# Three of four token parts of a final RMSNorm summed by a matrix of ones, and the scaling moved into the last matmul chains

## The chip, the cores and the metric

The kernel runs on one core of one Trainium2 chip. The metric is the device time of one execution in microseconds, as the median of several runs. One execution was also profiled; its trace is what the argument works from.

## The reference, cut to what matters

One decoder layer (attention with a 128-token window, a gated MLP branch, a ConvFFN) for 1024 prompt tokens and 64 sample tokens, and a final RMSNorm. The part that the change touches is the end:

```python
def rmsnorm(x, g):
    xf = x.astype(jnp.float32)
    y = xf * lax.rsqrt(jnp.mean(xf * xf, axis=-1, keepdims=True) + EPS)
    return (y * g.astype(jnp.float32)).astype(x.dtype)
...
    x = x + merged @ w_out
    f, nconv = conv_ffn(rmsnorm(x, norm_ffn), w_up, conv_w, conv_b, w_down, conv_prev)
    return x + f, nk, nv, nconv, vn
...
    y_prompt = rmsnorm(xp, norm_final)
    y_sample = rmsnorm(xs, norm_final)
```

D is 1024, the ConvFFN is 2816 wide, everything is float32.

## The kernel before, in words

Activations lie transposed: 128 channels on the partitions, tokens along the free axis. The 1088 tokens (64 sample, 1024 prompt) are two halves of 544 (`th` 0 and 1); the 1024 channels are 8 tiles of 128, in two halves of 4 tiles (`dh` 0 and 1, tile `m` 0 to 3 in each). To keep float32 accuracy every operand is split into a rounded high plane and a low rest (`split`, line 41: ScalarE copies the high plane, VectorE subtracts), and each product is three matmuls: high by high, high by low, low by high.

**Up-projection.** Two-by-two block products are done with seven instead of eight products (`Chain.product`, line 310). Token group 0 (576 tokens, two halves of 288 columns) reads four T tiles `t0` to `t3`, each `[128, 7, 2, 288]` with seven sums and their two planes; group 1 (two halves of 256 columns) reads `th`/`tl` tiles. The T tiles of group 0 come from `both_planes`, one tile at a call, with 64 bytes of gap (`line(pool, 64)`) behind each. A tile is 16128 bytes, 63 times 256, so one gap of 64 shifts a tile's start by 64 against a multiple of 256. They are made twice, for the input projection and for the up-projection.

**Down-projection.** Again seven products in the order `DN_ORDER = (5, 0, 2, 4, 6, 1, 3)`, here called stages 0 to 6. Each stage has 11 units (`NU`); a unit is a half weight tile (`wh`, `wl`, 128x512) and a token operand (`th`, `tl`, 128x544), and gives 24 matmuls (4 tiles `m`, two column spans `e` of 288 and 256, three terms; `mm_dn`, line 1679). `units` asks ahead: it has token operands split up to unit x+2 and weights split two units ahead of the one in use (`W.get(2, ...)`). A stage's sums are in six PSUM banks `dn` and are taken into the residual `x1[dh, th, e]` on VectorE (`take`, line 1689). Token half 0 is complete after stage 4, half 1 with channel half 1 after stage 5, and the last stage finishes half 1 with channel half 0.

**The last four units** run as chains: span e=0 with m 0 to 3, each 12 matmuls, then span e=1 likewise. A chain's end lets `take` and the squares (`square`, line 1698) follow.

**Final norm.** It is done for four parts `(th, e)`. `square` sums squares over channel tiles into `acc` (VectorE, line 1701). `fin_rms` (line 1712) reduces over the partitions with small matmuls (`acc` as weights, one column of ones), takes the root on ScalarE and the reciprocal of a few columns on VectorE; `fin_rb` (line 1724) spreads the result over the partitions by matmuls with an identity; `fin_mul` copies that to SBUF (ScalarE, line 1732) and multiplies: VectorE with the gain from PSUM (line 1749), GpSimd from SBUF (line 1751). Parts (0,0) and (0,1) are reduced ahead of unit 8 of stage 5 and unit 0 of stage 6, and multiplied ahead of units 2 and 3 of stage 6 (`hooks[at, lo]`). Part (1,0) is reduced and multiplied inside the e=1 chains. Part (1,1) comes last, with three matmuls of ones ahead of its end (line 1837). Every part leaves by DMAs from the SyncE queue (`y_out`, line 1737).

A scheduler orders the instructions of each engine. An instruction under `tc.keep_in_program_order` keeps its place among the others so marked.

Of the kernel before, what the change touches and what calls it, by code (L numbers as in the profile page):

```python
# [15 lines left out]
P = 128  # L16
D = 1024
KD = 8
# [16 lines left out]
def layer(tc, a):  # L35
    nc = tc.nc
    V, S, G, PE = nc.vector, nc.scalar, nc.gpsimd, nc.tensor
# [11 lines left out]
    with ExitStack() as top:  # L49
# [12 lines left out]
        eps = cst.tile([P, 1], F32, name="c_eps")  # L62
# [182 lines left out]
        W = Weights(top.enter_context(tc.tile_pool(name="wp", bufs=2)), 4, 4)  # L245
# [16 lines left out]
        def both_planes(pool, name):  # L262
            t = pool.tile([P, 7, 2, 288], F32R, name=name)
            line(pool, 64)
            return t[:, :, 0], t[:, :, 1]

        def combine(t4, b11, b12, b21, b22, eng=G):
# [108 lines left out]
        with ExitStack() as ph1:  # L376
            c1 = ph1.enter_context(tc.tile_pool(name="c1", bufs=1))
# [61 lines left out]
            early = set(range(NPRE, FEW))  # L439
# [199 lines left out]
            t0h, xr = right(th0, "T0h"), right(xro, "xr")  # L639
            txa = [{}, {}]  # L640
# [20 lines left out]
            def t0_job(kk):  # L661
                def go():
                    first, t4, rest = sums_of(0, kk)
                    txa[0][kk] = th, tl = both_planes(t0h, f"t{kk}")
# [287 lines left out]
            for at, (pair, gs) in enumerate(seq):  # L952
# [12 lines left out]
                for j in range(7):  # L965
                    w = W.get(3, 1 if j < 4 else 4 if at == len(seq) - 1 else 2)
# [407 lines left out]
            for c in range(KD):  # L1374
                xt = x_next(0, c)
                w, ps = W.get(), acc2()
# [9 lines left out]
            t0p = right(t0o, "T0")  # L1386
# [38 lines left out]
            def t0_split(kk):  # L1425

                def go():
                    x0, x1, t4 = hx.pop(kk)
                    tx[0][kk] = th, tl = both_planes(t0p, f"t0{kk}")
# [24 lines left out]
        def t_upto(loads, splits):  # L1454

            for n in range(len(ts["raw"]), min(loads, 7 * (NFF // 2))):
                j, i = DN_ORDER[n // (NFF // 2)], n % (NFF // 2)
                raw = dnp["t"].tile([P, 576], F32, name="traw", bufs=4)[:, :HT]
                nc.sync.dma_start(raw, td[i][:, T_AT[j]])
                ts["raw"].append(raw)  # L1460
            for n in range(len(ts["made"]), min(splits, 7 * (NFF // 2))):
                th, tl = (dnp["t"].tile([P, 576], F32R, name=x, bufs=5)[:, :HT] for x in ("th", "tl"))
                if n == 0:
                    line(dnp["t"], 128)
                split(th, tl, ts["raw"][n])
                ts["made"].append((th, tl))
# [187 lines left out]
        with ExitStack() as ph3:  # L1654
# [48 lines left out]
            def fin_rms(th, e, more=()):  # L1703

                lo, hi = spans[e]
                nb = 3 - e
                m = (hi - lo) // nb
                ps = psl.tile([P, 512], F32, name="fs", bufs=2)
                parts = (acc[th][:, lo:hi], *more)
                for k, x in enumerate(parts):  # L1710
                    for i in range(nb):
                        PE.matmul(ps[0:m, 320 + i:321 + i], x[:, i * m:i * m + m], ones[:, 0:1],
                                  start=i + k == 0, stop=k == len(parts) - 1, skip_group_check=True)
# [5 lines left out]
            def fin_rb(ps, rt, nb, m, both=False):  # L1719

                both = [ps] + ([psl.tile([P, 512], F32, name="fs", bufs=2)] if both else [])
                for p in both:
                    for i in range(nb):
                        PE.matmul(p[:, i * m:i * m + m], rt[:, i:i + 1].to_broadcast([m, P]), ident[0:m, 0:m],
                                  start=True, stop=True)
                return [p[:, :nb * m] for p in both]

            def fin_mul(th, e, rb, last=False):
                lo, hi = spans[e]
                w, at = hi - lo, KD * (HT * th + lo)  # L1730
                rs = lp.tile([P, 288], F32, name="rb", bufs=2)[:, :w]
                S.copy(rs, rb[-1])
                rb = rb[0]

                def y_out(c0, c1):
                    tc.keep_in_program_order(
                        nc.sync.dma_start(a["y"][:, at + c0 * w:at + c1 * w].rearrange("p (m t) -> p m t", t=w),
                                          x1[c0 // 4, th, e][:, c0 % 4:c0 % 4 + c1 - c0]))

                if last:  # L1740
                    for c in range(0, KD, 2):
                        x2, eng, by = x1[c // 4, th, e][:, c % 4:c % 4 + 2], V if c < 6 else G, rb if c < 6 else rs
                        eng.tensor_mul(x2, x2, by[:, None, :].to_broadcast([P, 2, w]))
                        y_out(c, c + 2)
                    return
                for c in range(KD):
                    xc = x1[c // 4, th, e][:, c % 4]
                    if c < 4:
                        V.scalar_tensor_tensor(xc, xc, gains[:, 2, c:c + 1], rb, ALU.mult, ALU.mult)
                    else:  # L1750
                        G.tensor_mul(xc, xc, rs)
                    if c in (3, 7):
                        y_out(c - 3, c + 1)
# [10 lines left out]
            def units(n, count):  # L1764
                out = []
                for x in range(n, n + count):
                    t_upto(x + 5, x + 3)
                    w = W.get(2, 5 if W.more else 3)
                    out.append((w, ts["made"][x]))
                return out  # L1770

# [9 lines left out]
            hooks[5, 7] = [lambda: [fin_scale(1, 0, m, e) for m in range(4) for e in range(2)]]  # L1781
            hooks[6, 6] = [lambda: [fin_scale(1, 1, m, e) for m in range(4) for e in range(2)]]
            fin = {}
            for at, lo, e in ((5, 8, 0), (6, 0, 1)):
                hooks[at, lo] = [lambda e=e: fin.update({e: fin_rms(0, e)})]
# [52 lines left out]
            fin_mul(1, 1, fin_rb(*fin[3], True), True)  # L1838
        tops.close()
        tops.close()  # L1840

# [90 lines left out]
```

## Time and profile before

| what | value |
|---|---|
| median of 3 runs | 1511.06 us (1510.43 to 1516.56) |
| the profiled execution | 1511.13 us, its span 1509.4 us, mean granted clock 0.999 |
| TensorE busy | 1493.9 us, 99% of the span |
| VectorE busy | 1175.3 us, 78% |
| ScalarE busy | 851.9 us, 56% |
| GpSimd busy | 267.9 us, 18% |
| last chains and norm (from 1484.8 us) | TensorE's last down-projection matmul starts at 1499.2 us; the span ends at 1509.4 us |

The time outside the span is 1.7 us. A row of the timeline gives the start in the span, the time from the start of the first to the end of the last of its instructions, engine, line, operation, output and inputs, and the shape; "x2" are two merged instructions, and a bracket at the end is the idle time of the engine before them and what ended it. A matmul's own duration overlaps the next one's, so the pace of TensorE is read from start to start.

### The profile page before, as it was taken

The numbers are of one execution on the slowest core, as the hardware profiler recorded it, in microseconds if no ns is written. First come the engines' busy times: TensorE is split into PE (matmuls) and PEld (weight loads), VectorE is DVE, ScalarE is ACT, GpSimd is POOL, SyncE is SP. The second block draws the span as 40 slices with busy tenths as digits, with TensorE's granted clock in tenths as the row PEclk, the third lists the DMA queues.
The fourth block names the chain that finished last, engine by engine and source line by source line (L and its number), as shares of the span: only waits on it lengthen the run. The fifth ranks groups of instructions, "written<-read, shape, count | busy, mean of one in ns | idle before, by whom it ended". The sixth has DMA issues, their size and how long they took to land.

```text
span 1509.4 us, 30138 instructions
## 1 busy us (share of the span) xinstructions
PE 1493.9 (99%) x11538; PEld 1454.6 (96%) x11538; DVE 1175.3 (78%) x1892; ACT 851.9 (56%) x1778; POOL 267.9 (18%) x381
## 2 busy tenths in 40 slices
PE   9999999999999999999999999999999999999998
PEld 9999999999998989998989999999999999999998
DVE  7798877755576877979667988898899888685686
ACT  8557676654455765864453555555555556353463
POOL 0001000010030222320134422332142222000002
PEclk9999999999999999999999999999999999999999
DMA  7688446864779757438988323332232216983463
GB/s 257 220 275 273 153 164 223 254 211 143 244 234 291 217 178 233 159 130 303 334 297 289 134 107 122 116 124 108 101 133 109 102 65 236 328 288 103 113 186 126
DMA packets 134431, 289.88 MB, mean 192 GB/s; under 512 B 15760, under 2 KB 36560, under 8 KB 134288
## 3 DMA queue, kind: packets, MB, share of 16 engines
q1 hardware_dynamic: 134144, 287.96, 56.9%
q8 instruction: 90, 1.47, 0.4%
q14 instruction: 53, 0.43, 0.1%
q10 hardware_dynamic: 144, 0.01, 0.0%
HBM read 198.97 MB, written 90.92 MB: 192 GB/s over the span
## 4 chain that ended last, share of the span: by engine, by line
PE 81%; DVE 6%; ACT 4%; DMA 4%; issue 3%; POOL 1%; SPq 0%; POOLq 0%; ACTq 0%; DVEq 0%
PE st L310 43%; PE dn L1679 13%; PE mm L242 13%; PE st L528 7%; PE po L1226 2%; PE sc L1175 2%; DVE wl L41 1%; DMA stg<-sd 1%; PE pt L1202 1%; DMA v<-gvd 1%; ACT wh L41 1%; PE mx L809 1%; ACT s L1192 1%; DMA kd<-q 0%; DMA stg<-vnd 0%
## 5 line engine op out<-in xcount | busy, mean ns | idle before, releaser
L310 PE MATMUL st<-t,wh 128*128 128x288 f32 x2128 | 428.6, 294 | 3.0 <-ACT k L289 1.6
L310 PEld LDWEIGHTS st<-t,wh 128*128 128x128 f32 x2128 | 335.9, 188 | 4.0 <-ACT k L289 2.2
L310 PE MATMUL st<-t,wl 128*128 128x288 f32 x1064 | 312.5, 294 | 0.0
L310 PE MATMUL st<-th,wh 128*128 128x256 f32 x1064 | 295.5, 278 | 1.9 <-ACT k L289 1.8
L310 PE MATMUL st<-tl,wh 128*128 128x256 f32 x1064 | 294.2, 277 | 0.0
L310 PE MATMUL st<-th,wl 128*128 128x256 f32 x1064 | 293.9, 276 | 0.0
L310 PEld LDWEIGHTS st<-th,wh 128*128 128x128 f32 x1064 | 199.8, 188 | 3.3 <-ACT k L289 2.9
L310 PEld LDWEIGHTS st<-th,wl 128*128 128x128 f32 x1064 | 199.9, 188 | 0.0
L310 PEld LDWEIGHTS st<-t,wl 128*128 128x128 f32 x1064 | 199.8, 188 | 0.0
L310 PEld LDWEIGHTS st<-tl,wh 128*128 128x128 f32 x1064 | 199.7, 188 | 0.0
L1679 PE MATMUL dn<-th,wh 128*128 128x288 f32 (+1 forms) x616 | 176.9, 287 | 0.8 <-ACT zb L336 0.6
L1679 PE MATMUL dn<-tl,wh 128*128 128x288 f32 (+1 forms) x616 | 176.2, 286 | 0.0
L1679 PE MATMUL dn<-th,wl 128*128 128x288 f32 (+1 forms) x616 | 175.2, 284 | 0.2 <-DVE wl L41 0.2
L41 ACT CAST wh<-wraw 128x512 fp32r<-128x512 f32 (+2 forms) x188 | 129.5, 701 | 81.2 <-DMA wraw<-wt 34.2
L41 DVE TENSOR_TENSOR wl<-wraw,wh 128x512 fp32r<-128x512 f32 (+2 forms) x188 | 148.6, 804 | 30.3 <-ACT wh L41 28.2
L41 ACT CAST wh<-ws 128x512 fp32r<-128x512 f32 x168 | 102.6, 621 | 95.4 <-PE st L310 58.1
L41 DVE TENSOR_TENSOR wl<-ws,wh 128x512 fp32r<-128x512 f32 x168 | 119.1, 719 | 44.3 <-ACT wh L41 43.4
L1679 PEld LDWEIGHTS dn<-th,wh 128*128 128x128 f32 x616 | 115.6, 188 | 1.3 <-ACT zb L336 0.9
L1679 PEld LDWEIGHTS dn<-th,wl 128*128 128x128 f32 x616 | 115.9, 188 | 0.4 <-DVE wl L41 0.4
L1679 PEld LDWEIGHTS dn<-tl,wh 128*128 128x128 f32 x616 | 115.7, 188 | 0.0
L528 PE MATMUL st<-w2h,hh 128*128 128x256 f32 x288 | 80.5, 280 | 0.4 <-ACT rst L494 0.4
L528 PE MATMUL st<-w2l,hh 128*128 128x256 f32 x288 | 80.0, 278 | 0.0
(277 smaller groups left out, 3165.1 us busy)
## 6 DMA issues: line engine op xcount, KB each, us to landing
wraw<-wt SPq DMA_DIRECT2D x137, 512.0 KB
traw<-td SPq DMA_DIRECT2D x77, 272.0 KB
td<-za SPq DMA_DIRECT2D x22, 544.0 KB
q<-qd SPq DMA_DIRECT2D x16, 512.0 KB
upd<-hl SPq DMA_DIRECT2D x14, 512.0 KB
td<-t SPq DMA_DIRECT2D x11, 544.0 KB
wpart<-wt SPq DMA_DIRECT2D x22, 256.0 KB
qd<-q SPq DMA_DIRECT2D x8, 576.0 KB
```

What stands on the lines that cost most here:

```text
L41: for x in (S.copy(hi, src), V.tensor_sub(lo, src, hi.bitcast(F32))):
L242: PE.matmul(ps[:, lo:lo + c1 - c0], u[:, k, :], v[:, c0:c1], start=(k == 0 and i == 0), stop=(k == nk - 1 and i == 2))
L310: PE.matmul(ps, u[:, kk, :], v, start=first and kk + i == 0, stop=kk == 3 and i == 2, skip_group_check=True)
L528: PE.matmul(ps, u[:, lo:lo + P], v[:, k, :], start=k + i == 0, stop=k == KD - 1 and i == 2)
L809: PE.matmul(ps[:, P * i:P * i + P], vn[:, i], late["wst"][:, c, :], start=True, stop=True)
L1175: PE.matmul(ps[:, h, o0:256], q, kst[kv][:, e, k0:cur + P], start=e == 0, stop=e == 1)
L1192: S.activation(s[:, h], s[:, h], AF.Exp, bias=nm[:, h:h + 1], accum_out=dn[:, h:h + 1])
L1202: PE.transpose(pt[:, h * P:h * P + P], s[:, h, 0:P], ident)
L1226: PE.matmul(po, v[:, kv, :], t, start=e == 0, stop=last)
L1679: PE.matmul(place(m, e), u[:, m, :], v[:, lo:hi], start=new and i + k == 0 and (e == 0 or m % 2 == 0), stop=i == NU - 1 and k == 2, skip_g ...
```

## The change

Two things. First, the places of the T tiles: all four of a set are now allocated when the first is asked for, in the order 2, 0, 1, 3, with 64 bytes of gap ahead of 2, 0 and 3 and none ahead of 1, and 64 behind the last. Against a multiple of 256 bytes, from the place of the first tile before, tiles 0 to 3 stood at 0, 64, 128 and 192; they now stand at 128, 128, 64 and 192. The sum of the space is the same.

Second, the final norm of parts (0,0), (0,1) and (1,0). `fin_rows` multiplies a 128x128 matrix of ones by `acc` (and, for (1,0), by the last square), which sums over the partitions and spreads the sum at once; root and reciprocal then run over all 288 or 256 columns. The gains are no longer in VectorE's multiplication; ScalarE applies them ahead (`fin_scale`) to every tile. `fin_mul` now takes two channel tiles in one instruction, on VectorE for channel tiles 0 to 3 and on GpSimd for 4 to 7. The multiplications of (0,0) and (0,1) and their DMAs move from stage 6 into the last units' chains (after m=0 and m=1 of e=0), and VectorE's of (1,0) behind the last takes. For the last six units `units` asks one unit further ahead. Part (1,1) is computed as before.

```diff
+        planes = {}
+
+        def both_planes(pool, name, kk):
+            if kk == 0:
+                for x, gap in ((2, 64), (0, 64), (1, 0), (3, 64)):
+                    if gap:
+                        line(pool, gap)
+                    planes[x] = pool.tile([P, 7, 2, 288], F32R, name=f"{name}{x}")
+                line(pool, 64)
+            t = planes.pop(kk)
             return t[:, :, 0], t[:, :, 1]
...
+            def fin_rows(th, e, more=()):
+
+                lo, hi = spans[e]
+                ps = psl.tile([P, 512], F32, name="fs", bufs=2)[:, :hi - lo]
+                parts = (acc[th][:, lo:hi], *more)
+                for k, x in enumerate(parts):
+                    PE.matmul(ps, ones, x, start=k == 0, stop=k == len(parts) - 1)
+                rt = lp.tile([P, 288], F32, name="rw", bufs=1)[:, :hi - lo]
+                S.activation(rt, ps, AF.Sqrt, bias=eps, scale=1.0 / D)
+                V.reciprocal(ps, rt)
+                return [ps]
...
+            def fin_mul(th, e, by, cs, eng=V):
+                w = spans[e][1] - spans[e][0]
+                for c in cs:
+                    x2 = x1[c // 4, th, e][:, c % 4:c % 4 + 2]
+                    x = eng.tensor_mul(x2, x2, by[:, None, :].to_broadcast([P, 2, w]))
+                    if eng is V:
+                        tc.keep_in_program_order(x)
...
-                    t_upto(x + 5, x + 3)
-                    w = W.get(2, 5 if W.more else 3)
+                    early = x >= 7 * NU - 6
+                    t_upto(x + 5, x + 3 + early)
+                    w = W.get(2 + early, 5 if W.more else 3)
...
-            for at, lo, e in ((6, 2, 0), (6, 3, 1)):
-                hooks.setdefault((at, lo), []).append(lambda e=e: fin_mul(0, e, fin_rb(*fin[e])))
...
                     if e and m == 0:
-                        fin[2] = fin_rms(1, 0, last)
-                    elif e and m == 1:
-                        fin_mul(1, 0, fin_rb(*fin[2]))
+                        rb, rs = fin_copy(1, 0, fin_rows(1, 0, last))
+                        fin_mul(1, 0, rs, (4, 6), G)
                     for m2 in (m - 1, m) if m % 2 and e else () if e else (m,):
                         take(3, m2, e)
                         sqs.append(square(0, 1, m2, e, False, m2 < 3 and not e))
-                        if e:
-                            fin_scale(0, 1, m2, e)
+                        fin_scale(0, 1, m2, e)
+                    if not e and m < 2:
+                        rb, rs = fin_copy(0, m, fin[m])
+                        fin_mul(0, m, rs, (4, 6), G)
+                        fin_mul(0, m, rb, (0, 2))
+                        for c in (0, 4):
+                            y_out(0, m, c, c + 4)
                 last = sqs if e else sqs[3:]
+            fin_mul(1, 0, rb, (0, 2))
+            for c in (4, 0):
+                y_out(1, 0, c, c + 4)
             fin[3] = fin_rms(1, 1, last)
```

VectorE's order from the last weight split to its end, before (`x_17062` is the residual of channel half 0 and token half 1, `x_17487` that of channel half 1, `x_16747` that of channel half 0 and token half 0, `acc_16746` the sum of squares of token half 1, `dn` a bank of products):

```order
L41 TENSOR_TENSOR wl<-wpart,wh 128x512
L1689 TENSOR_TENSOR x_17062<-x_17062,dn 128x288
L1701 TENSOR_TENSOR acc_16746<-acc_16746,sq 128x288
L1689 TENSOR_TENSOR x_17062<-x_17062,dn 128x288
L1701 TENSOR_TENSOR acc_16746<-acc_16746,sq 128x288
L1689 TENSOR_TENSOR x_17062<-x_17062,dn 128x288
L1701 TENSOR_TENSOR acc_16746<-acc_16746,sq 128x288
L1689 TENSOR_TENSOR x_17062<-x_17062,dn 128x288
L1716 RECIPROCAL rt<-rt 96x3
L1689 TENSOR_TENSOR x_17062<-x_17062,dn 128x256 x2
L1749 TENSOR_SCALAR x_17062<-x_17062,c_gains,fs 128x288 x4
L1689 TENSOR_TENSOR x_17062<-x_17062,dn 128x256 x2
```

The same place on VectorE in the changed kernel:

```order
L41 TENSOR_TENSOR wl<-wpart,wh 128x512
L1696 TENSOR_TENSOR x_17062<-x_17062,dn 128x288
L1708 TENSOR_TENSOR acc_16746<-acc_16746,sq 128x288
L1696 TENSOR_TENSOR x_17062<-x_17062,dn 128x288
L1765 TENSOR_TENSOR x_16747<-x_16747,fs 128x576 x2
L1708 TENSOR_TENSOR acc_16746<-acc_16746,sq 128x288
L1765 TENSOR_TENSOR x_16747<-x_16747,fs 128x512 x2
L1696 TENSOR_TENSOR x_17062<-x_17062,dn 128x288 x2
L1708 TENSOR_TENSOR acc_16746<-acc_16746,sq 128x288
L1744 RECIPROCAL fs<-rw 128x288
L1696 TENSOR_TENSOR x_17062<-x_17062,dn 128x256 x4
L1765 TENSOR_TENSOR x_17062<-x_17062,fs 128x576 x2
```

The multiplications of (0,0) and (0,1) stand between the takes of m=1 and m=2, the sum of squares of m=1 between them; a reciprocal over 288 columns stands ahead of the four takes of e=1, and the multiplications of (1,0) behind them.

TensorE at the norm of part (1,0) in the e=1 chains, before (`fs` is the bank of the norm):

```order
L1679 MATMUL dn<-tl,wh 128x256
L1679 MATMUL dn<-th,wl 128x256
L1712 MATMUL fs<-c_ones,acc_16746 96x1 x3
L1712 MATMUL fs<-c_ones,sq 96x1 x3
L1679 MATMUL dn<-th,wh 128x256
L1679 MATMUL dn<-tl,wh 128x256
```

And in the changed kernel:

```order
L1686 MATMUL dn<-th,wl 128x256
L1686 MATMUL dn<-th,wh 128x256
L1741 MATMUL fs<-acc_16746,c_ones 128x288
L1741 MATMUL fs<-sq,c_ones 128x288
L1686 MATMUL dn<-tl,wh 128x256
L1686 MATMUL dn<-th,wl 128x256
```

Two products by ones replace six small ones, and stand four matmuls further on (behind 16 of e=1, where the small ones stood behind 12); three spreading products by the identity, which stood 12 matmuls behind the small ones, are gone.

More of the change, by code (lines that the diff above doesn't have):

```diff
@@ L260, in right @@
             return stack.enter_context(tc.tile_pool(name=name, bufs=bufs, side="right", reuse_waits="tile"))
-        def both_planes(pool, name):
-            t = pool.tile([P, 7, 2, 288], F32R, name=name)
-            line(pool, 64)
+        planes = {}
[7 more added lines that the diff above has]
+            t = planes.pop(kk)
             return t[:, :, 0], t[:, :, 1]
@@ L663, in go @@
                     first, t4, rest = sums_of(0, kk)
-                    txa[0][kk] = th, tl = both_planes(t0h, f"t{kk}")
+                    txa[0][kk] = th, tl = both_planes(t0h, "t", kk)
                     split(th[:, 0], tl[:, 0], first)
@@ L1428, in go @@
                     x0, x1, t4 = hx.pop(kk)
-                    tx[0][kk] = th, tl = both_planes(t0p, f"t0{kk}")
+                    tx[0][kk] = th, tl = both_planes(t0p, "t0", kk)
                     split(th[:, 0], tl[:, 0], x0[:, 0:288])
@@ L1717, in fin_rms, with fin_rb @@
                 return ps, rt, nb, m
-            def fin_rb(ps, rt, nb, m, both=False):
-                both = [ps] + ([psl.tile([P, 512], F32, name="fs", bufs=2)] if both else [])
+            def fin_rb(ps, rt, nb, m):
+                both = [ps, psl.tile([P, 512], F32, name="fs", bufs=2)]
                 for p in both:
@@ L1726, in fin_rb @@
                 return [p[:, :nb * m] for p in both]
-            def fin_mul(th, e, rb, last=False):
+            def fin_rows(th, e, more=()):
[8 more added lines that the diff above has]
+                return [ps]
@@ L1729, in fin_mul, with y_out @@
+            def y_out(th, e, c0, c1):
                 lo, hi = spans[e]
                 w, at = hi - lo, KD * (HT * th + lo)
[L1731 to L1753, printed above, removed]
+                tc.keep_in_program_order(
+                    nc.sync.dma_start(a["y"][:, at + c0 * w:at + c1 * w].rearrange("p (m t) -> p m t", t=w),
+                                      x1[c0 // 4, th, e][:, c0 % 4:c0 % 4 + c1 - c0]))
@@ new lines, in fin_copy @@
+            def fin_copy(th, e, rb):
+                rs = lp.tile([P, 288], F32, name="rb", bufs=2)[:, :spans[e][1] - spans[e][0]]
+                copy = S.copy(rs, rb[-1])
+                if not (th and e):
+                    tc.keep_in_program_order(copy)
+                return rb[0], rs
+            def fin_mul(th, e, by, cs, eng=V):
[5 more added lines that the diff above has]
+                        tc.keep_in_program_order(x)
@@ L1780, in layer @@
                     hooks[at, 2 + m] = [squares(*q, m, first and m == 0)]
-            hooks[5, 7] = [lambda: [fin_scale(1, 0, m, e) for m in range(4) for e in range(2)]]
+            hooks[5, 7] = [lambda: [fin_scale(dh, 0, m, e) for dh in range(2) for m in range(4) for e in range(2)]]
             hooks[6, 6] = [lambda: [fin_scale(1, 1, m, e) for m in range(4) for e in range(2)]]
@@ L1784, in layer @@
             for at, lo, e in ((5, 8, 0), (6, 0, 1)):
-                hooks[at, lo] = [lambda e=e: fin.update({e: fin_rms(0, e)})]
-            for at, lo, e in ((6, 2, 0), (6, 3, 1)):
-                hooks.setdefault((at, lo), []).append(lambda e=e: fin_mul(0, e, fin_rb(*fin[e])))
+                hooks[at, lo] = [lambda e=e: fin.update({e: fin_rows(0, e)})]
             for at, j in enumerate(DN_ORDER):
@@ L1837, in layer @@
                 PE.matmul(bank[0][:, 0:P], ones, ones, start=True, stop=True)
-            fin_mul(1, 1, fin_rb(*fin[3], True), True)
+            rb, rs = fin_copy(1, 1, fin_rb(*fin[3]))
+            for c in range(0, KD, 2):
+                fin_mul(1, 1, *((rb, (c,), V) if c < 6 else (rs, (c,), G)))
+                y_out(1, 1, c, c + 2)
         tops.close()
```

## The prediction

> **What bounds the kernel now.** I read the page first, then the chain of work that ended last, the order in time of TensorE around the last units, VectorE's and GpSimd's order there, and the table of stretches for the transfers at the end. The page says that TensorE is the bound of nearly the whole span:
>
> ```profile
> span 1509.4 us, 30138 instructions
> PE 1493.9 (99%) x11538; PEld 1454.6 (96%) x11538; DVE 1175.3 (78%) x1892; ACT 851.9 (56%) x1778; POOL 267.9 (18%) x381
> L310 PE MATMUL st<-t,wh 128*128 128x288 f32 x2128 | 428.6, 294 | 3.0 <-ACT k L289 1.6
> L310 PE MATMUL st<-t,wl 128*128 128x288 f32 x1064 | 312.5, 294 | 0.0
> ```
>
> So an edit counts where TensorE waits or streams less, or behind its last product. The chain that ended last (start, length, what) shows which engine is late near the end:
>
> ```profile
> 1486.33 0.70 DVE wl L41
> 1487.04 0.04 issue
> 1487.08 6.52 PE dn L1679 x49
> ...
> 1497.33 3.10 POOL x L1751 x4
> ```
>
> Up to 1487.0 the weight splits on VectorE are the late ones, then TensorE. TensorE's order in time at the last unit's weights shows what that costs; successive starts of undisturbed 288-column products are 0.13 apart:
>
> ```profile
> 1485.88 0.29 PE L1679 MATMUL dn<-th,wl 128*128 128x288 f32 x1
> 1486.35 0.40 PE L1679 MATMUL dn<-th,wh 128*128 128x288 f32 x1 [0.18 <-ACT wh L41]
> 1486.59 0.29 PE L1679 MATMUL dn<-tl,wh 128*128 128x288 f32 x1
> 1487.08 0.40 PE L1679 MATMUL dn<-th,wl 128*128 128x288 f32 x1 [0.19 <-DVE wl L41]
> ```
>
> From start to start 0.47 and 0.49 instead of 0.13: 0.34 + 0.36 = 0.70 us lost there. Everything else in this part of the span that TensorE does is streaming, so the change can earn these 0.70 us, the norm's own products, and what follows TensorE's end.
>
> **The norm's products on TensorE.** The rows of part (1,0) before, and of an earlier product by the matrix of ones (576 columns in two pieces, each recorded in two passes):
>
> ```profile
> 1493.44 0.59 PE L1712 MATMUL fs<-c_ones,acc 128*96 128x1 f32 x6
> 1493.89 0.65 PE L1712 MATMUL fs<-c_ones,sq 128*96 128x1 f32 x6
> 1494.40 0.36 PE L1679 MATMUL dn<-th,wh 128*128 128x256 f32 x1
> 1494.60 0.28 PE L1679 MATMUL dn<-tl,wh 128*128 128x256 f32 x1
> ...
> 1495.89 0.81 PE L1724 MATMUL fs<-c_ident,rt 96*128 96x96 f32 x6
> 1496.48 0.37 PE L1679 MATMUL dn<-th,wh 128*128 128x256 f32 x1
> ```
> ```profile
> 770.32 1.13 PE L1399 MATMUL mm<-rs,c_ones 128*128 128x320 f32 x4
> 771.36 0.47 PE L242 MATMUL mm<-mh,wh 128*128 128x512 f32 x1
> ```
>
> The 576 columns held TensorE from 770.32 to 771.36, 1.04 us, so 288 columns cost 0.52 and 256 cost 0.46. Before, six sums cost 0.45 (1493.44 to 1493.89) and six spreading records 0.59 (1495.89 to 1496.48). Part (0,0): 0.45 + 0.59 - 0.52 = 0.52 saved. Part (0,1) has four records where the others have six, two thirds: 0.69 - 0.46 = 0.23 saved. Part (1,0): 0.96 (1493.44 to 1494.40) + 0.59 - 2 x 0.52 = 0.51 saved. After such an insertion the first down-projection product takes 0.20 to the next start (1494.40 to 1494.60), 0.08 more than the pace of 0.115 to 0.12 of 256 columns; each part has one insertion fewer: 3 x 0.08 = 0.24. Together 1.50 us, of which 0.52 + 0.23 + 0.16 = 0.91 ahead of the last units' chains.
>
> **The weight splits ahead of the last chains.** VectorE gains two reciprocals and loses eight multiplications, and GpSimd's eight leave this place. VectorE's load there, and the prices (the reciprocal's row gives nanoseconds):
>
> ```profile
> 1455.50:1487.10 31.60, 31.23 (x252) 30.76 (x250) 28.20 (x52) 18.15 (x38) 7.33 (x8) 1.00 0.47 160
> L1401 DVE RECIPROCAL rs<-rs x1: 3753/3753/3753, 774.0 to 774.0; 128x576 f32<-128x576 f32 x1
> 1470.28 1.78 DVE L1749 SCALAR_TENSOR_TENSOR x<-x,c_gains,fs 128x288 f32<-128x288 f32 x4
> 1474.25 1.65 DVE L1749 SCALAR_TENSOR_TENSOR x<-x,c_gains,fs 128x256 f32<-128x256 f32 x4
> 1471.76 0.80 POOL L1751 TENSOR_TENSOR x<-x,rb 128x288 f32<-128x288 f32 x1
> 1471.98 1.14 DVE L41 TENSOR_TENSOR wl<-wpart,wh 128x512 fp32r<-128x512 f32 x1
> 1480.52 0.68 DVE L41 TENSOR_TENSOR wl<-wpart,wh 128x512 fp32r<-128x512 f32 x1
> ```
>
> A reciprocal over 576 columns took 3.75 us, so 288 cost 1.88 and 256 cost 1.67: 3.55 us more, against 1.78 + 1.65 = 3.43 less. But `wl` took 1.14 us beside GpSimd and 0.68 without, and VectorE has several such operations with two inputs in SBUF there; those surcharges (0.46 on this one) leave the place too. VectorE thus has no more to do ahead of the last units than the 28.2 of 31.6 us it has, and the last six units are asked for one unit earlier. The reciprocals come at about 1455 and 1464, where weights are split units ahead of use; that is their cover. If it were gone, they would cost up to their 3.55 us. I take the 0.70 us of waiting as gone. The first take of e=0, at 1487.52 before, comes 0.91 + 0.70 = 1.61 earlier, at 1485.9. ScalarE's twelve added gains of about half a microsecond lie in its idle time (18.15 of 31.6 us busy there); the sqrt over 288 columns is bounded by the row of 576 below.
>
> **The queue in the last chains.** Here the change adds work on VectorE that stands ahead of what TensorE waits for. The prices:
>
> ```profile
> 773.19 0.74 ACT L1400 ACTIVATE rs<-mm,c_eps 128x576 f32<-128x576 f32 x1
> 1487.52 0.45 DVE L1689 TENSOR_TENSOR x<-x,dn 128x288 f32<-128x288 f32 x1 [0.49 <-PE dn L1679]
> 1488.00 0.45 ACT L1698 ACTIVATE sq<-x 128x288 f32<-128x288 f32 x1 [1.71 <-DVE x L1689]
> 1488.48 0.46 DVE L1701 TENSOR_TENSOR acc<-acc,sq 128x288 f32<-128x288 f32 x1 [0.51 <-ACT sq L1698]
> 1503.56 1.88 DVE L1743 TENSOR_TENSOR x<-x,fs 128x512 f32<-128x512 f32 x3 [0.80 <-PE fs L1724]
> 1504.51 1.27 POOL L1743 TENSOR_TENSOR x<-x,rb 128x512 f32<-128x512 f32 x1 [4.08 <-ACT rb L1732]
> ```
>
> A VectorE multiplication is 1.88 / 3 = 0.63 for 512 columns, so 0.70 for 576; GpSimd's is 1.27, so 1.43 for 576. The walk, from the take at 1485.9: square, gain and copy of the factor on ScalarE (about 0.45, 0.5 and 0.4) let GpSimd start at about 1487.75, its two for (0,0) ending at 1489.2 and 1490.6. VectorE: sum of m=0 done at 1487.3, take of m=1 (one chain of 1.58 later) 1487.9, two multiplications 1489.3. Now comes the sum of m=1, with both inputs in SBUF while GpSimd works. In the rows above `wl` started at 1471.98 inside GpSimd's 1471.76 to 1472.56 and ended at 1473.12, 0.56 after GpSimd's end, less than its 0.68 alone: it waited for that instruction to end. So the sum waits to 1490.6 and is done at 1490.95. Then two multiplications (1.26) to 1492.2, takes of m=2 and m=3 to 1493.0, and the sum of m=2 ready at 1493.1, which falls into GpSimd's fourth instruction (1492.2 to 1493.5): done at about 1493.8. TensorE reaches the product by ones at 1493.44 - 1.61 + 4 x 0.115 = 1492.3 and, being in order, holds all of e=1's remaining 32 matmuls behind it. It waits 1.5 us. Without any blocking the second sum would be done at 1492.4 (wait 0.1); with the surcharge of 0.46 on each sum, at 1493.3 (1.0). I take 1.5, by the rows' times, and keep 0.1 for the range.
>
> The Trainium skill says in "SBUF — State Buffer", "Who interferes with whom", that VectorE with two SBUF inputs and a reading GpSimd exclude each other for a whole instruction, the second blocking fully; it speaks against GpSimd's wider instructions here. The row of `wl` (1.14 against 0.68) agrees; by the rule the wait is 1.5, by a shared-speed reading 1.0.
>
> TensorE's end is thus 1.50 + 0.70 - 1.5 = 0.70 earlier. The reciprocal of (1,0), 1.9 us ahead of the takes of e=1, hides under the 32 matmuls (3.7 us); uncovered it would delay the end by what it lacks.
>
> **Behind TensorE's end.** Part (1,1) is as before and moves with it. Its output shares the DMA engines with that of (1,0) (after POOL's column: granted clock, DMA share, GB/s):
>
> ```profile
> 1501.00:1502.00 1.00, 1.00 (x12) 1.00 (x11) 0.00 (x0) 0.50 (x2) 0.00 (x0) 1.00 1.03 415
> 1503.00:1504.00 1.00, 0.97 (x8) 0.78 (x7) 0.44 (x1) 0.00 (x0) 0.00 (x0) 1.00 0.00 0
> 1506.00:1507.00 1.00, 0.00 (x0) 0.00 (x0) 0.00 (x0) 0.00 (x0) 0.00 (x0) 0.50 1.01 385
> ```
>
> Before, the 1.18 MB of (1,0) were through by 1503, an idle microsecond lay between, and the last 1.05 MB followed. Now VectorE's two multiplications of (1,0) stand behind the last takes; with both halves issued at about 1501, 0.8 to land at the engines and 1.18 MB at 415 GB/s (2.85 us), they are through at about 1504.7, 0.2 after the last part's first bytes could start. So 0.2 of the 0.70 is given back: 0.5 us gained.
>
> **The T tiles.** Four tiles are read one after another in each of 3192 / 12 = 266 group-0 products. One such product and the group-1 product behind it:
>
> ```profile
> 1150.38 0.42 PE L310 MATMUL st<-t,wh 128*128 128x288 f32 x2
> ...
> 1151.57 0.42 PE L310 MATMUL st<-t,wh 128*128 128x288 f32 x2
> ...
> 1151.96 0.28 PE L310 MATMUL st<-th,wh 128*128 128x256 f32 x1
> ...
> 1153.32 0.42 PE L310 MATMUL st<-t,wh 128*128 128x288 f32 x2
> ```
>
> Twelve matmuls of 288 columns take 1.58, twelve of 256 take 1.36; at the latter's pace a column the former would take 1.53. The last tile's three take 0.39, the three tiles before 1.19, 0.397 each. So moving the tiles can gain at most 0.05 x 266 = 13.3 us, and the rows show no place that is read at a pace other than 0.39 to 0.40; all four at 0.40 would be 1.60, 0.02 x 266 = 5.3 us lost. The values at hand are nearest to no difference, and I take zero, with 0.01 us a product (2.7 us) either way as what these rounded rows can hide.
>
> Sum: 1511.13 - 0.5 = 1510.6 us. The profiled execution lies 0.07 above the median of 1511.06, so I leave it at **1510.6**.
>
> **The rivals.**
>
> - *The sums are not blocked.* TensorE waits 0.1 instead of 1.5, and gains 1.85 at the end after the transfers' 0.2 or so: 1509.3. For it: before, these sums had GpSimd beside them only once. Against it: the row of `wl`. 15%.
> - *The reciprocals make the splits late.* Idle time on VectorE is only 3.4 of 31.6 us, and the 3.55 us come before the relief at 1470. If the last `wl` ends later than 1486 the chains of e=0 wait; with the reciprocals half uncovered 1.8 us are lost: 1512.4. 12%.
> - *The T tiles read slower*, two of them now on one place against a multiple of 256: 1510.6 + 2.7 = 1513.3 with half of the bound, 1515.9 with all. It decides when twelve matmuls take over 1.58. 10%.
> - *The T tiles read faster*: half of the gap to the 256-column pace is 6.6 us, 1504.0; all of it 1497.3. For it: the 0.05 us are there and nothing else in the rows explains them. 8%.
>
> **How the numbers follow.** The forecast has the remaining 55%. The range goes from the first rival less the hidden 2.7 us, 1506.6, to the forecast plus 2.7, 1513.3; it leaves out about half of each T rival. A measurement of this kernel can tell about 0.5%, 7.6 us, from no change. Faster by more than that needs over half of the T bound: 0.04. Slower by more needs the whole T loss with the late splits: 0.02. Within: 0.94.
>
> **What would show it.** Right: no gap at the last unit's `wh` and `wl`; the products by ones at 0.52 each; a sum of squares on VectorE beside GpSimd of about 1 us or more; TensorE idle ahead of the product by ones of (1,0) for 1 to 1.5 us; the DMA engines busy without a break in the last 6 us; twelve T matmuls at 1.58. Wrong: a gap at the last splits, no wait at the ones, or a pace of the T matmuls other than 1.57 to 1.59.

## The result, and the profile after

The changed kernel took 1507.61 us (median of 11 runs, 1505.34 to 1509.5) against 1511.07 for the kernel before (11 runs): ratio 0.9967, 95% interval 0.9952 to 0.9982. The quotient of the medians is 0.9977; the ratio agrees with that of the means, 1507.54 to 1512.54 us, which four of the 11 runs before, at 1514.5 to 1517.2, pull apart. The forecast was 1510.6, a gain of 0.5 us; the gain was 3.5 us by the medians and 5.0 by the means (2.7 to 7.3 by the interval). The time is inside the range (1506.6 to 1513.3) and the change inside "within 0.5%", but even the smaller gain is seven times what the sum had said.

The page of the changed kernel, the two rows that answer to those of before:

```profile
span 1505.9 us, 30082 instructions
PE 1491.5 (99%) x11508; PEld 1451.8 (96%) x11508; DVE 1176.4 (78%) x1886; ACT 856.3 (57%) x1790; POOL 265.7 (18%) x375
```

TensorE is still the bound, so the question is where it lost less. The trace cuts well at the first down-projection product. The rows of its high-by-high products (minimum, median and maximum duration in ns, then first and last start) for before, and for the changed kernel:

```profile
L1679 PE MATMUL dn<-th,wh x616: 276/289/402, 1266.5 to 1499.0; 128*128 128x288 f32 x150, 128*128 128x256 f32 x4
```
```profile
L1686 PE MATMUL dn<-th,wh x616: 275/295/509, 1265.3 to 1495.2; 128*128 128x288 f32 x150, 128*128 128x256 f32 x4
```

From there to the end of the span it was 1509.4 - 1266.5 = 242.9 us before and 1505.9 - 1265.3 = 240.6 now: 2.3 us of the gain lie in the down-projection and the norm, the rest ahead of it.

**The stall at the last unit is gone.** TensorE's order in time at the last unit's `wh` and `wl`, where 0.47 and 0.49 us had stood from start to start:

```profile
1483.37 0.29 PE L1686 MATMUL dn<-th,wl 128*128 128x288 f32 x1
1483.50 0.30 PE L1686 MATMUL dn<-th,wh 128*128 128x288 f32 x1
1483.63 0.30 PE L1686 MATMUL dn<-tl,wh 128*128 128x288 f32 x1
1483.77 0.29 PE L1686 MATMUL dn<-th,wl 128*128 128x288 f32 x1
```

**The products by ones** of (0,0), and, in the last chains, of (1,0):

```profile
1451.80 0.29 PE L1686 MATMUL dn<-th,wl 128*128 128x288 f32 x1
1451.92 0.65 PE L1741 MATMUL fs<-acc,c_ones 128*128 128x288 f32 x2
1452.19 0.51 PE L1686 MATMUL dn<-th,wh 128*128 128x288 f32 x1
1452.54 0.30 PE L1686 MATMUL dn<-tl,wh 128*128 128x288 f32 x1
...
1490.36 0.28 PE L1686 MATMUL dn<-th,wh 128*128 128x256 f32 x1
1490.76 0.75 PE L1741 MATMUL fs<-acc,c_ones 128*128 128x288 f32 x2
1491.35 0.65 PE L1741 MATMUL fs<-sq,c_ones 128*128 128x288 f32 x2
1491.62 0.49 PE L1686 MATMUL dn<-tl,wh 128*128 128x256 f32 x1
1491.95 0.28 PE L1686 MATMUL dn<-th,wl 128*128 128x256 f32 x1
```

The first insertion holds TensorE from 1451.92 to 1452.54, of which 0.13 is the step of the down-projection product behind it: 0.49 us, the late restart of that product included. Ahead of the second TensorE is late by 1490.76 - 1490.36 - 0.115 = 0.28 us. That is the new wait; 1.5 us had been forecast.

**VectorE and GpSimd at that place.** The rows of the sums of squares (L1708) and of GpSimd's multiplications, from the order in time of the two engines, each instruction by itself:

```profile
1486.02 1.43 POOL L1765 TENSOR_TENSOR x<-x,rb 128x576 f32<-128x576 f32 x1 [220.51 <-ACT rb L1756]
1487.38 0.46 DVE L1708 TENSOR_TENSOR acc<-acc,sq 128x288 f32<-128x288 f32 x1
1487.41 1.71 POOL L1765 TENSOR_TENSOR x<-x,rb 128x576 f32<-128x576 f32 x1
1489.09 1.29 POOL L1765 TENSOR_TENSOR x<-x,rb 128x512 f32<-128x512 f32 x1
1489.91 0.80 DVE L1708 TENSOR_TENSOR acc<-acc,sq 128x288 f32<-128x288 f32 x1
```

The sum of m=1 started at 1487.38, 0.03 ahead of GpSimd's second instruction and 0.07 before the recorded end of its first, and took 0.46 us, as it does alone. GpSimd paid: its second instruction took 1.71 us where its first had taken 1.43. The sum of m=2 did start inside GpSimd's third (1489.09 to 1490.38) and took 0.80.

**The end.** The transfers in the last microseconds (last three columns: granted clock, DMA share, GB/s):

```profile
1498.00:1499.00 1.00, 0.56 (x6) 0.47 (x5) 0.11 (x1) 0.26 (x1) 0.00 (x0) 1.00 0.30 124
1499.00:1500.00 1.00, 0.89 (x8) 0.89 (x8) 0.20 (x2) 0.00 (x0) 0.00 (x0) 1.00 0.98 401
1503.00:1504.00 1.00, 0.00 (x0) 0.00 (x0) 0.00 (x0) 0.00 (x0) 0.00 (x0) 0.50 0.97 379
```

From 1499 to 1504 every microsecond has a share of 0.97 to 1.02: the idle microsecond between the two parts' bytes is gone, as forecast.

### The profile page after: what moved, and what is told of

Read it like the earlier page. It is cut to its first block, busy times and chain, and to the rows that moved or that the text cites. A ratio compares the mean times of both kernels' runs of the same rounds, so it can differ in the third digit from the quotient of the medians.

```text
span 1505.9 us, 30082 instructions
## 1 busy us (share of the span) xinstructions
PE 1491.5 (99%) x11508; PEld 1451.8 (96%) x11508; DVE 1176.4 (78%) x1886; ACT 856.3 (57%) x1790; POOL 265.7 (18%) x375
## 4 chain that ended last, share of the span: by engine, by line
PE 85%; DVE 5%; ACT 4%; DMA 3%; issue 2%; POOL 1%; SPq 0%; POOLq 0%; ACTq 0%; DVEq 0%
PE st L317 45%; PE dn L1686 14%; PE mm L242 13%; PE st L535 6%; PE po L1233 2%; PE sc L1182 1%; DVE wl L41 1%; PE pt L1209 1%; DMA v<-gvd 1%; PE mx L816 1%; ACT wh L41 1%; ACT s L1199 1%; DMA kd<-q 0%; DMA v<-gvds 0%; DVE v L761 0%
## 5 line engine op out<-in xcount | busy, mean ns | idle before, releaser
L535 PE MATMUL st<-w2h,hl 128*128 128x256 f32 x288 | 80.1, 279 | 0.1
```

The source lines that it names most:

```text
L535: PE.matmul(ps, u[:, lo:lo + P], v[:, k, :], start=k + i == 0, stop=k == KD - 1 and i == 2)
```

## The experiments

Where no interval stands, a time is one run; 23 runs of the kernel before on one chip lie between 1508.09 and 1515.65 us, so two such times are not compared. Besides the time, two lengths of each trace are used: from the first down-projection product to the end of the span ("down and norm"), and the number of matmuls that the profile counts in the 400 us from 850 to 1250, which lie wholly in the up-projection ("count"; more is faster).

**T places alone.** The kernel before with the new `both_planes` of the diff and nothing else.

> The kernel before with the T tiles' new places alone; the norm is as before. Theory: the changed kernel's gain of 3.5 us has a part from the T tiles: the median product of twelve 288-column matmuls goes from 1.577 to 1.570 us in its trace, 266 of them, so 1 to 2 us of the time, and nothing at the end of the span moves (the last down-projection matmul to the span's end stays at 10.2 us). Rival: the places do nothing, the product stays at 1.577 and the time within 0.5 us of the kernel before; the whole gain is the norm's.

**Norm alone.** The changed kernel with the old `both_planes`.

```diff
-            if kk == 0:
-                for x, gap in ((2, 64), (0, 64), (1, 0), (3, 64)):
...
+            t = pool.tile([P, 7, 2, 288], F32R, name=name)
+            line(pool, 64)
```

> The changed kernel with the T tiles at their old places. Theory: twelve T matmuls are back at 1.577 us, and the end keeps what the changed kernel's trace shows against before: 1.2 us at the sums of parts (0,0) and (0,1), 1.2 us in the last units' chains; time 2 to 2.5 us below the kernel before. Rival (T tiles do nothing): 3.5 us below. Rival (the norm's part is as I forecast): 0.5 us below.

T alone: 1510.35 us against 1512.03, ratio 0.9988 (0.9978 to 0.9998). Norm alone: 1509.87, ratio 0.9991 (0.9979 to 1.0004). Each ratio is too near to one to size a part, but the traces do. The stretch from 850 to 1250 (the number behind the first busy time is the count) for before, norm alone, the changed kernel and T alone:

```profile
850.00:1250.00 400.00, 399.90 (x3273) 399.34 (x3272) 347.43 (x489) 221.94 (x444) 109.51 (x162) 1.00 0.31 111
```
```profile
850.00:1250.00 400.00, 399.90 (x3273) 399.35 (x3272) 348.96 (x494) 222.50 (x444) 111.92 (x160) 1.00 0.31 111
```
```profile
850.00:1250.00 400.00, 399.90 (x3280) 399.35 (x3279) 346.44 (x490) 222.07 (x444) 111.31 (x162) 1.00 0.30 111
```
```profile
850.00:1250.00 400.00, 399.90 (x3278) 399.36 (x3277) 348.87 (x494) 222.41 (x444) 110.07 (x160) 1.00 0.31 112
```

The old places give 3273 twice, the new ones 3280 and 3278: 5 to 7 matmuls more in 400 us, each of about 0.122 us, so 0.6 to 0.9 us. The start times of the trace show the same for single products: the twelve 288-column matmuls of one take 1576 to 1577 ns in the median with the old places (before, norm alone) and 1570 in all five traces with the new ones (T alone, changed, and three of the kernels below), in the input projection as in the up-projection. That is 1.8 us over 266 products: 1.0 us in the 154 of the up-projection and 0.8 in the 112 of the input projection.

Down and norm is 242.9 and 243.1 us with the old norm (before, T alone), 240.5 and 240.6 with the new one (norm alone, changed kernel). So the norm is worth 2.3 to 2.6 us wherever the T tiles stand, and the T tiles about 1.0 us of the up-projection. The first up-projection product starts at 807.8 to 811.8 us in kernels with the same T places, so whether the 0.8 us of the input projection reaches the time can't be read from one trace; the ratio of T alone, 1.8 us (0.3 to 3.3), fits the whole 1.8.

**The look-ahead.** I had put the vanished stall down to two edits together, the asking of the last units one unit earlier and the removal of GpSimd's work.

```diff
-                    early = x >= 7 * NU - 6
+                    early = 0
```

> The changed kernel, the last six units asked for no further ahead than the others. Theory: part of the 0.9 us that TensorE lost at the last unit's weights before comes back: the last wl split ends 0.5 to 1.4 us later than in the changed kernel against TensorE's first e=0 product, and TensorE shows a gap of 0.2 to 0.7 us. Rival: the splits were late only because GpSimd's multiplications stood beside them, which have moved; then no gap appears and the time is that of the changed kernel.

1507.86 us; down and norm 1506.1 - 1265.4 = 240.7, as in the changed kernel. TensorE's order in time at the last unit, and the last weight split on VectorE:

```profile
1482.58 0.69 DVE L41 TENSOR_TENSOR wl<-wpart,wh 128x512 fp32r<-128x512 f32 x1 [0.69 <-ACT wh L41]
1483.60 0.29 PE L1686 MATMUL dn<-th,wl 128*128 128x288 f32 x1
1483.73 0.29 PE L1686 MATMUL dn<-th,wh 128*128 128x288 f32 x1
1483.87 0.30 PE L1686 MATMUL dn<-tl,wh 128*128 128x288 f32 x1
1484.00 0.29 PE L1686 MATMUL dn<-th,wl 128*128 128x288 f32 x1
```

No gap either, with the last split done 0.7 us ahead of its first use. With the T places alone both gaps are still there:

```profile
1487.74 0.40 PE L1686 MATMUL dn<-th,wh 128*128 128x288 f32 x1 [0.19 <-ACT wh L41]
1488.47 0.40 PE L1686 MATMUL dn<-th,wl 128*128 128x288 f32 x1 [0.19 <-DVE wl L41]
```

The look-ahead is not needed; the norm's changes without it take the stall away. That it is GpSimd's absence beside the splits rather than VectorE's own changed work (3.43 us of multiplications left this place as well) is argued, not shown by itself: before, a `wl` beside GpSimd took 1.05 to 1.14 us, and now all of them in the last units take 0.68 to 0.69.

**A wider instruction on GpSimd.** For (0,0) and (0,1) GpSimd multiplies four tiles in one instruction instead of two twice, so that the sum of m=1 must start inside it.

```diff
-                        fin_mul(0, m, rs, (4, 6), G)
+                        x4 = x1[1, 0, m][:, 0:4]
+                        G.tensor_mul(x4, x4, rs[:, None, :].to_broadcast([P, 4, spans[m][1] - spans[m][0]]))
```

> The changed kernel, GpSimd's two multiplications of parts (0,0) and (0,1) each as one instruction over four channel tiles (1152 and 1024 columns), about 2.85 and 2.55 us long. Theory (a VectorE sum with two inputs in SBUF waits for GpSimd's whole instruction, and the changed kernel escaped by a tie, its sum of m=1 starting 0.07 us ahead of an instruction's end): the sum of m=1 now ends 1.3 us later than in the changed kernel, that of m=2 1.3 to 1.5 us later, and TensorE waits 1.5 to 1.8 us instead of 0.28 ahead of the products by ones; span 1 to 1.5 us longer. Rival (the two share a port's speed): each sum takes 0.8 instead of 0.46 and TensorE waits under 0.8 us.

1507.06 us, down and norm 1505.4 - 1263.6 = 241.8, 1.2 more than the changed kernel. The rows (GpSimd, VectorE, TensorE):

```profile
1484.28 2.67 POOL L1848 TENSOR_TENSOR x<-x,rb 128x1152 f32<-128x1152 f32 x1 [220.43 <-ACT rb L1756]
1485.64 1.62 DVE L1708 TENSOR_TENSOR acc<-acc,sq 128x288 f32<-128x288 f32 x1
1488.62 0.28 PE L1686 MATMUL dn<-th,wh 128*128 128x256 f32 x1
1489.89 0.75 PE L1741 MATMUL fs<-acc,c_ones 128*128 128x288 f32 x2 [0.99 <-DVE acc L1708]
```

The sum of m=1 now takes 1.62 us, to 0.31 behind GpSimd's end at 1486.95, and TensorE waits 1489.89 - 1488.62 - 0.115 = 1.16 us. The sum of m=2 is not blocked here (0.50 us); it is late because the sum of m=1 is. This is the wait of the prediction, by its mechanism, at three quarters of its size and under the 1.5 to 1.8 us expected of this kernel. In the changed kernel the condition is missed by 0.03 us, and not by the chance of one run: in all eight kernels here that have these instructions at this place, the sum of m=1 starts 0.02 to 0.03 us ahead of GpSimd's second and TensorE waits 0.27 to 0.28 us.

**All four T tiles at one place.** In the trace of before, three of the twelve steps from one 288-column matmul to the next took 128 ns and the others 131 to 134, which I put down to the place of the operand against a multiple of 256 bytes. Four kernels (the changed one with no gaps between the tiles, and a gap of 0, 64, 128 or 192 ahead of the first) put the tiles at one place each; the edit for 64:

```diff
-                for x, gap in ((2, 64), (0, 64), (1, 0), (3, 64)):
+                for x, gap in ((0, 64), (1, 0), (2, 0), (3, 0)):
...
-                line(pool, 64)
+                line(pool, 192)
```

> The changed kernel with all four T tiles at the place of tile 0 before (0 against a multiple of 256 bytes), no gap between them. Theory (a T matmul's pace depends on where its plane starts; in the traces before and after, the start-to-start time behind a matmul whose plane starts 192 bytes on from that first place, or 64 for a high plane's low neighbour at 192, is 128 ns, behind the others 132 to 133): a tile's three matmuls read planes at 0, 128, 0, so 132 + 132.4 + 132 each, twelve in about 1.585 us. Rival (the pace depends on the step from one tile to the next, not on the place): equal steps make all four such kernels alike.

> The same with all four T tiles at 64. Theory: planes at 64, 192, 64, so 133 + 128.4 + 133 each, twelve in about 1.578 us. Rival: like the other three kernels.

> The same with all four T tiles at 128. Theory: planes at 128, 0, 128, so 132.4 + 132 + 132.4 each, twelve in about 1.587 us. Rival: like the other three kernels.

> The same with all four T tiles at 192. Theory: planes at 192, 64, 192, so 128.4 + 133 + 128.4 each, twelve in about 1.559 us, the fastest of the four, 0.011 us less than in the changed kernel, 3 us over 266 products. Rival: like the other three kernels.

The number of matmuls from 850 to 1250, the mean step of a matmul in the products of the up-projection, and the median of the twelve 288-column matmuls, worked out from their start times (times of one run each, before on the same chip; of the changed kernel the median above; the count and the steps of before are those of its trace above; the four have the new norm):

| kernel | time, us | count | step, 288 columns, ns | step, 256 columns, ns | twelve of 288, ns |
|---|---|---|---|---|---|
| before | 1512.69 | 3273 | 131.4 | 114.0 | 1577 |
| changed | 1507.61 | 3280 | 130.85 | 114.0 | 1570 |
| gap 0 | 1514.62 | 3238 | 131.75 | 116.2 | 1581 |
| gap 64 | 1517.86 | 3210 | 134.6 | 115.6 | 1616 |
| gap 128 | 1518.93 | 3220 | 132.9 | 116.5 | 1582, 1608 |
| gap 192 | 1510.47 | 3258 | 132.5 | 114.1 | 1590 |

The place theory fell: the place that should have been the best gave 1590 where 1559 was expected, and that of 64 gave 1616 where 1578 was. Its rival fell too, for the four kernels are not alike. One product of the kernel with gap 64, in which all four tiles stand at the same place:

```profile
1151.35 0.43 PE L317 MATMUL st<-t,wh 128*128 128x288 f32 x2
...
1151.74 0.43 PE L317 MATMUL st<-t,wh 128*128 128x288 f32 x2
...
1152.15 0.45 PE L317 MATMUL st<-t,wh 128*128 128x288 f32 x2
...
1152.57 0.43 PE L317 MATMUL st<-t,wh 128*128 128x288 f32 x2
...
1152.97 0.28 PE L317 MATMUL st<-th,wh 128*128 128x256 f32 x1
```

The tiles take 0.39, 0.41, 0.42 and 0.40 us: the same place costs differently by its turn. By the count all four arrangements are slower than either kernel's, and in three of them the 256-column products, whose tiles were not moved, are slower as well.

With gap 128 the twelve matmuls take 1608 and 1582 ns by turns, from one product to the next. Two products in a row, each from its first matmul to the first of the 256-column ones behind it:

```profile
1149.56 0.43 PE L317 MATMUL st<-t,wh 128*128 128x288 f32 x2
...
1151.16 0.28 PE L317 MATMUL st<-th,wh 128*128 128x256 f32 x1
...
1152.54 0.42 PE L317 MATMUL st<-t,wh 128*128 128x288 f32 x2
...
1154.12 0.28 PE L317 MATMUL st<-th,wh 128*128 128x256 f32 x1
```

1.60 and 1.58 us, with the T tiles where they are and read in the same order. So something else that changes from product to product enters as well. The weight tile, which stands in another buffer each time, is one candidate; no run here moves it.

**The same places in another order.** The gaps of the changed kernel, with the tiles in the order 0, 1, 2, 3.

```diff
-                for x, gap in ((2, 64), (0, 64), (1, 0), (3, 64)):
+                for x, gap in ((0, 64), (1, 64), (2, 0), (3, 64)):
```

> The changed kernel with its T tiles at the same four places, but kept in the order 0, 1, 2, 3 instead of 2, 0, 1, 3: tile 0 now stands at place 32 mod 256, 1 and 2 at 96, 3 at 160. If the pace of the products follows the set of places, the twelve products stay at 1570 ns and the stage from the last mixing product to the first of the down stage at 442.0 to 442.3 us. If it follows the sequence in which places are read, as the four kernels with all tiles at one place suggest (a tile at the same place took 131 to 143 ns for the same product, by its turn), it comes out elsewhere in 1570 to 1616 ns, the stage 442 to 450 us, and the time moves with it.

1508.27 us; the twelve products take 1583 ns, and the row of the stretch from 850 to 1250 is

```profile
850.00:1250.00 400.00, 399.91 (x3266) 399.35 (x3265) 345.93 (x487) 220.50 (x441) 111.18 (x162) 1.00 0.31 111
```

3266 against 3280 is 14 matmuls, 1.7 us, lost by the order alone; down and norm is unchanged at 240.8. So the set of places does not decide the pace. Which tile stands at which place does, whether through the sequence in which the places are read or through what each tile meets there, its weights for one, is not separated. By what rule stays open.

**A version with three edits at the end.**

```diff
+                        if not e and m == 3:
+                            rb, rs = fin_copy(0, 1, fin[1])
+                            fin_mul(0, 1, rs, (4, 6), G)
+                            y_out(0, 1, 4, 8)
...
-                    if not e and m < 2:
-                        rb, rs = fin_copy(0, m, fin[m])
...
+                    if not e and m == 0:
+                        rb, rs = fin_copy(0, 0, fin[0])
...
-            for c in (4, 0):
-                y_out(1, 0, c, c + 4)
+            for c in (4, 0, 2, 6):
+                y_out(1, 0, c, c + 2)
...
-            for _ in range(3):
+            for _ in range(1):
```

> The changed kernel with three edits of its end. (1) The copy of (0,1)'s reciprocal, and with it GpSimd's two multiplications of that part, start behind the square of the first half's m=3, at about 1490.7 of the changed kernel's time instead of 1489.1, so that no GpSimd instruction stands beside VectorE's sum of m=2: if that sum waits for GpSimd, it takes 0.46 instead of 0.80 us and the gap ahead of the product by ones of (1,0) goes from 0.40 to 0.12 (-0.28); if the sum was long for another reason, nothing. (2) y of (1,0) leaves in four pieces of two channels in the order in which they are ready, the first at about 1496.5 instead of 1497.9; its 1.18 MB and the 1.05 MB of the last part kept the DMA engines busy from 1498.7 to 1504.3, so if their bytes bound the end, the stretch from the last square sums' products to the end falls from 8.28 us by 0.5 to 1.3; if the last part's own chain bounds it, by at most 0.2. (3) One product ones by ones ahead of the last square sums instead of three: their start moves from 1497.61 to about 1497.15 (-0.45) unless the clock falls for it. Sum: the stretch behind 1448.6 from 58.4 to about 57.0 (range 56.3 to 58.0), the time about 1.2 to 2 us under the changed kernel's, ratio to the kernel before about 0.996. If edit 3 lowers the granted clock, the small products behind it become slower and the end comes out as it was.

1506.81 us against 1511.94, ratio 0.9975 (0.9965 to 0.9984) where about 0.996 was expected. Down and norm is 1503.9 - 1264.4 = 239.5 us, 1.1 less than in the changed kernel where about 1.4 was expected of the end. VectorE's sums, GpSimd, TensorE and the transfers:

```profile
1489.09 0.46 DVE L1708 TENSOR_TENSOR acc<-acc,sq 128x288 f32<-128x288 f32 x1
1489.67 0.69 PE L1741 MATMUL fs<-acc,c_ones 128*128 128x288 f32 x2
1490.19 2.53 POOL L1765 TENSOR_TENSOR x<-x,rb 128x512 f32<-128x512 f32 x2 [1.87 <-ACT rb L1756]
1495.58 0.47 PE L1864 MATMUL dn<-c_ones 128*128 128x128 f32 x2
1495.88 0.95 PE L1719 MATMUL fs<-c_ones,sq 128*128 128x1 f32 x8
1499.00:1500.00 1.00, 0.00 (x0) 0.00 (x0) 1.00 (x2) 0.01 (x1) 0.91 (x1) 0.50 0.54 210
```

With GpSimd kept away the sum of m=2 takes 0.46 instead of 0.80, and the product by ones follows without a wait. From there to the last square sums' products it takes 1495.88 - 1489.67 = 6.21 us, against 1497.61 - 1490.76 = 6.85 in the changed kernel, with one product ones by ones in place of three. The granted clock stayed at 1.00 until these products were through. From the last square sums' products to the end it takes 8.02 us instead of 8.28, near what was expected if the last part's own chain is the bound and not its bytes (0.2 less), and the DMA engines have idle time again (share 0.54). The two versions were not timed against each other, and their ratios to the kernel before, 0.9975 and 0.9967, do not show this one faster; that its end is shorter by about 1 us is read from the traces.

## Why the prediction was right or wrong

- *Direction and range*: right. *Size*: 0.5 forecast, 3.5 measured (medians). Two terms failed, the new wait and the T tiles, and two were mis-sized the same way.
- *The new wait of TensorE, 1.5 us*: the step that failed most. It took 0.28. That VectorE and GpSimd exclude each other held; what failed was the walk of starts to which it was applied. From the first take it put GpSimd's second instruction at 3.3 us and the sum of m=1 at 3.4, inside it; they came at 3.31 and 3.28. VectorE's queue was the part in error: its prices were lengths of rows, and successive rows overlap, so that its two multiplications took 1.33 us from start to start and not 1.4. The wider instruction shows 1.16 us of wait for the same sum behind it. The rival "not blocked", given 15% with 1509.3, was the nearer case. A walk good to a tenth of a microsecond can't decide a margin of 0.03, so that rival should have had about as much chance as the forecast. The Trainium skill's sentence on this ("SBUF — State Buffer", "Who interferes with whom": the second of the two blocks fully for the whole instruction) agrees with the runs whichever engine is second: 1.62 us for VectorE's sum in the kernel with the wider instruction, 1.71 us for GpSimd's multiplication here.
- *The T tiles, taken as zero*: failed. They give about 1.0 us in the up-projection and up to 0.8 in the input projection. The rows gave 0.39 to 0.40 a tile, and the effect is 7 ns in 1577; two decimals of one product can't show it, as the prediction's own 2.7 us either way said. The count of matmuls in a long stretch does, in one row.
- *The norm's products, 1.50 us*: right in kind, 1.83 measured. The insertion of (0,0) costs 0.49, its late restart included, and not 0.52 with 0.08 on top; before, the insertions of (0,0) and (0,1) had cost 2.10 together and now 0.91, those of (1,0) 1.72 and now 1.08.
- *The stall at the last unit, 0.70 us*: gone, worth 0.91, since the products behind each gap were slow to restart as well. The earlier asking of the last units, to which I had given part of this, does nothing here.
- *The reciprocals*: 1.96 us for 288 columns against 1.88 forecast; that of (1,0) ended at 1494.52, before TensorE's last product started at 1495.48, so it was hidden, as said, and the splits were not late.

```profile
1492.56 1.96 DVE L1744 RECIPROCAL fs<-rw 128x288 f32<-128x288 f32 x1 [1.86 <-ACT rw L1743]
```

- *The transfers, 0.2 given back*: right. The stretch from the last square sums' products to the end was 8.10 us before and is 8.28; from those products to the start of GpSimd's last multiplication it took 3.20 in both, so the difference lies in the transfers.
- Together: 1.83 + 0.91 - 0.28 - 0.18 = 2.28 us of the 2.3 in down and norm. With 1.0 to 1.8 of the T tiles that makes 3.3 to 4.1, against 3.5 by the medians and 5.0 by the means; the difference is within the interval and within what the stretch ahead of the up-projection varies by.

## What to carry to other kernels

Where two engines exclude each other, a wait worked out from a walk of starts can turn on hundredths of a microsecond: take the prices from start to start and not from the rows' lengths, give both outcomes a chance, and if the order matters, make it sure by what the second engine waits for. Count the instructions that start in a long, steady stretch before and after; a difference of 0.2% shows there in one row that the rounded rows of a single product do not show. A look-ahead and a removed rival for an engine may both seem to explain a stall that went; leaving out one of them costs one run.

## What was not expected of the hardware

The pace of fp32r matmuls, with TensorE busy for 399.9 of 400 us and the granted clock at 1.00, depended on where the moving tiles lie and on which of them lies where: the mean step of 288 columns went from 130.85 to 134.6 ns, and between the changed kernel and the one with gap 64 the stretch of 400 us lost 70 of 3280 matmuls, 2.1%. Neither the place of one tile nor the set of places decides it, and with gap 128 one and the same arrangement took 1608 and 1582 ns by turns. A VectorE instruction that starts just ahead of GpSimd's makes GpSimd's the long one: 1.71 us in place of 1.43.
